# Output projection of a two-layer trunk: raw weight loads over five places, and splits placed behind the scaling of probabilities

## The chip, the cores and the metric

The kernel runs on one core of one Trainium2 chip. The metric is device time in microseconds (us): the median of several runs of the whole kernel. A core has a matrix engine (PE, whose weight loads are shown apart as PEld), a vector engine (DVE), a scalar engine (ACT), GpSimd (POOL) and SyncE (SP). Each of them works off its own list of instructions in the order in which they were issued. Here SP only starts transfers from main memory.

## The reference, cut to what matters

The model is a decoder trunk of two layers over 512 positions of width 1024. Each layer is half a SwiGLU block, a mixer with 8 forgetting-attention ("Fox") heads and 4 differential heads, and another half SwiGLU block. Everything is float32.

```python
for layer in range(DEPTH):
    x = x + 0.5 * _swiglu(_rmsnorm(x, ffn1_norm[layer]), ...)
    h = _rmsnorm(x, mix_norm[layer])
    proj = h @ w_in                       # 1024 x 3080
    o_f, o_d = _causal_block_attention(...)   # 8 Fox heads, 4 differential heads
    x = x + concat([o_f, o_d]) @ w_out    # 1024 x 1024, the product that the change is about
    x = x + 0.5 * _swiglu(_rmsnorm(x, ffn2_norm[layer]), ...)
return _rmsnorm(x, final_norm)
```

## The kernel before, in words

**Split weights.** A float32 product is made of three products of a rounded format. Each operand is split into a high part, which is the operand rounded, and a low part, which is what the rounding left out. `split` (L87 to L90) makes them from a raw block of 128 x 1024: ACT copies it (L88), then DVE subtracts (L89). `mm3` (L450 to L455) issues the three matrix products: high x high (L453), high x low (L454) and low x high (L455). So the first product of a block needs only ACT's part of the split, and the second needs DVE's part as well.

**The stream of weight blocks.** All weight blocks lie in one list, `stream`, in the order of their use. `plain` (L204 to L219) describes a block of the mixer: `need` starts the load of its raw block into a named place (`raw_tag`) if that place isn't marked busy, and `make` splits it and gives the place back. `ensure` (L259 to L270) makes the next block and then asks the following blocks for their loads, each of them if it lies fewer than `early` steps ahead (here 3). For each layer the list holds 24 blocks of the input projection and 7 blocks of the output projection, in the order `OUT_K = (4, 5, 6, 7, 0, 1, 2)`; block 3 is loaded apart in `out_rest` (L1153 to L1178), into place R2. Raw blocks rotate through three places, R0, R1 and R2 (L248). The seven output blocks have R1, R2, R0, R1, R2, R0, R1. Splits of blocks 4 to 7 go into the four tiles `XA0` to `XA3`, which hold the input of the input projection until its last products have read them. Splits of blocks 0 to 2 go into ring tiles ("wg").

**The mixer.** Twelve units are worked off one after the other, the four differential heads (units 0 to 3) and then the eight Fox heads (units 4 to 11). The loop over `s` (L1222 to L1244) has four steps for each unit. In step `s = 4u + i`, `softmax_step` makes the scores of unit u for the i-th block of 128 queries (PE, L948 and L949), masks them (DVE, L981) and takes the exponential (ACT, L983). After every second block of a Fox head the probabilities are scaled by the reciprocal of their sums (L988 to L994). ACT does it, except for the first two blocks of Fox heads 4 to 7, where DVE does it (L992). So each of those heads has one pair of scalings on ACT, of 128 x 384 and 128 x 512, in its fourth step. `trans_step` transposes the probabilities of the unit five steps back (PE, L1016; split by L1019 and L1020), and `pv_step` multiplies them with the values six steps back (PE, L1053 and L1054), and then adds up the head's output (L1083, L1084) and, at every second head, splits it (L1035, L1036).

**The filler.** Between these steps `pace` lets a generator, `filler`, issue other products of PE: the rest of the input projection and then `out_early` (L1135 to L1151). How far it may be after each third of a step is given by a table, counted in matrix products:

```python
LEAD = 70
TARGET = [128, 228, 280, 334, 380, 466, 478, 512, 520, 552, 564, 594, 612]
```

The n-th number is the count at the end of unit n. `out_early` takes the blocks of `w_out` in the order 4, 5, 6, 7, 0, 1 for three of the four groups of outputs of the first half of positions (9 products for each block), then the fourth group (18 products), then block 2 for all four groups (12). `take_wo` calls `next_w`, so a block's `make` runs where its first product is issued. What is left is issued after the loop (L1247), and then `out_rest` follows.

**What sets the order.** The program is written down in the order of these calls, and a scheduler then places the instructions of each engine: the earliest in this written order goes first, but one whose inputs are there (by the scheduler's reckoning) may be placed ahead of earlier ones that still wait. So a split or a filler product can move ahead of attention work. `tc.issue_after(x)` keeps the instructions of a block behind instruction x in the list of x's engine; it adds no wait.

**Other users of the places.** `w0` and `w1` hold the outputs of the differential heads (`os_`, L711; two heads in each) until `one` (L1102 to L1107) has read them with DVE (L1106).

Of the kernel before, what the change touches and what calls it, by code (L numbers as in the profile page):

```python
# [52 lines left out]
def rf(t):  # L53
    return t.bitcast(F32)
# [3 lines left out]
def trunk(ctx, tc, xT, x, gains, gain_row, w_gu, w_dn, w_in, w_ff, w_out, fbias, lams, subln, consts, rope, out):  # L58
    nc = tc.nc
    act, dve, pool, pe, sp = nc.scalar, nc.vector, nc.gpsimd, nc.tensor, nc.sync  # L60
# [16 lines left out]
    def home(tag, shape, dt, name):  # L77
        return sb.tile(shape, dt, tag=tag, name=name, bufs=1)
# [8 lines left out]
    def split(src, hi, lo):  # L87
        act.copy(out=hi, in_=src)  # L88
        dve.tensor_tensor(out=lo, in0=src, in1=rf(hi), op=ALU.subtract)  # L89
        return hi, lo  # L90
# [7 lines left out]
    def ring_tile(tag, cols):  # L98
        g = home(tag, [P, 2, 1024], F32R, "wg")
        return g[:, 0, :cols], g[:, 1, :cols]  # L100

    def raw_tile(tag, cols, src):
        t = home(tag, [P, 1024], F32, "raw")
        w = min(step[0], cols)
        for o in range(0, cols, w):
            sp.dma_start(out=t[:, o:o + w], in_=src[:, o:o + w])
        return t[:, :cols]
# [5 lines left out]
    stream = []  # L113
# [54 lines left out]
    def push(units, i, ring):  # L168
        for early, need, make in units:
            tag = ring[i % 5]  # L170
            i += 1
            stream.append((tag, early, need, lambda make=make, tag=tag: make(tag)))
        return i
# [27 lines left out]
            return tags.get(b), src  # L201
        return forms(order, 1, cols, where)

    def plain(src, raw_tag, tag):  # L204
        got = []

        def need():
            if not got and raw_tag not in busy:
                busy.add(raw_tag)
                got.append(raw_tile(raw_tag, 1024, src))  # L210

        def make():
            need()
            busy.discard(raw_tag)
            if tag is None:
                w = xt_[len_x.pop(0)]
                return split(got[0], w[:, 0:1024], w[:, 1024:2048])
            return split(got[0], *ring_tile(tag, 1024))
        return tag, 3, need, make  # L219

    NCH = len(PARTS_OF[0])

    def parts_of(n):

        parts = [("u", 0)]
        for c in range(1, NCH):
            parts += [("u", c), ("d", c - 1)]
        parts[-1] = ("dd", NCH - 1)
        return parts

    def pair_units(n):
        own = {s: iter(dn_units(n, NCH - 2 + i, "".join(u[0] for u in PAIRS[n] if u[1] == s), i == 1))
               for i, s in enumerate("ab")}
        return [next(own[u[1]]) for u in PAIRS[n]]

    def part_order(kind, c):
        return FIRST if (kind, c) == ("u", 0) else STEADY

    xt_ = [None] * KP
    len_x = list(range(KP)) * DEPTH  # L240
    OUT_K = (4, 5, 6, 7, 0, 1, 2)
    for n in range(2 * DEPTH):
        l = n // 2
        if n % 2 == 1:
            for i in range(24 + len(OUT_K)):
                k = OUT_K[i - 24] if i >= 24 else None
                tag = MIX[l][i % 3] if i < 24 else None if k >= 4 else MIX[l][(i - 28) % 3]
                stream.append(plain(w_in[l, i] if i < 24 else w_out[l, k], f"R{(i + 1) % 3}", tag))  # L248
        r = 0
        for kind, c in parts_of(n):  # L250
            if (n, kind, c) != (0, "u", 0):
                r = push(pair_units(n) if kind == "dd" else
                         (gu_units if kind == "u" else dn_units)(n, c, part_order(kind, c)), r, RINGS[n])
# [69 lines left out]
    norm = {}  # L323
# [357 lines left out]
    def mixer(l, n_next, mid):  # L681
# [14 lines left out]
        def pr_tile(u, qb):  # L696
            w = (qb + 1) * P
            return pg[u % 2][:, PR[qb]:PR[qb] + w]

        def pm_tile():  # L700
            return pg[nxt("pm", 2)][:, 1280:1792]
# [241 lines left out]
        def scores(q1, kk, m, qb, q2=None):  # L943
            n = (qb + 1) * P
            w = max(n, 256)
            p = psum("b")
            own = slice(qb * P, n)
            pe.matmul(p[:, 0:w], q1[m][:, own], kk[m][:, 0, 0:w], start=True, stop=False)  # L948
            pe.matmul(p[:, 0:w], (q1[m] if q2 is None else q2)[:, own], kk[m][:, 1, 0:w], start=False, stop=True)  # L949
            return p  # L950

        def softmax_step(u, qb):
            kind, h = units[u]
            n = (qb + 1) * P
            if kind == "d":
                st = sm.tile([P, 6], F32, tag="st", name="st", bufs=6)
                q1, kk = qk[("d", h)]
                pm = []
                for m in range(2):
                    p = scores(q1, kk, m, qb)  # L960
                    e = pr_tile(u, qb) if m == 0 else pm_tile()
                    dve.tensor_tensor_reduce(out=e[:, 0:n], in0=p[:, 0:n], in1=maskw[:, S - n:S], op0=ALU.add,
                                             op1=ALU.min, scale=1.0, scalar=3.0e38, accum_out=st[:, m:m + 1])
                    act.activation(out=e[:, 0:n], in_=e[:, 0:n], func=AF.Exp, scale=-1.0, bias=st[:, m:m + 1],
                                   accum_out=st[:, 2 + m:3 + m])
                    pm.append(e)
                dve.reciprocal(out=st[:, 4:6], in_=st[:, 2:4])
                dve.tensor_tensor(out=st[:, 5:6], in0=st[:, 5:6], in1=nlam, op=ALU.mult)
                act.mul(out=pm[1][:, 0:n], in_=pm[1][:, 0:n], mul=st[:, 5:6])
                dve.scalar_tensor_tensor(out=pm[0], in0=pm[0], scalar=st[:, 4:5], in1=pm[1][:, 0:n],  # L970
                                         op0=ALU.mult, op1=ALU.add)
                probs[u].append(pm[0])
            else:
                q1, kk = qk[("f", h // 2)]
                fox_q(h)
                p = scores(q1, kk, h % 2, qb, fq[h])
                e = pr_tile(u, qb)
                if qb % 2 == 0:
                    fst["st"] = sm.tile([P, 3, 2], F32, tag="st", name="st", bufs=6)
                st, i = fst["st"], qb % 2  # L980
                dve.tensor_tensor_reduce(out=e, in0=p[:, 0:n], in1=maskw[:, S - n:S], op0=ALU.add, op1=ALU.min,  # L981
                                         scale=1.0, scalar=3.0e38, accum_out=st[:, 0, i:i + 1])
                act.activation(out=e, in_=e, func=AF.Exp, scale=-1.0, bias=st[:, 0, i:i + 1],  # L983
                               accum_out=st[:, 1, i:i + 1])
                probs[u].append(e)
                if i == 0:
                    return
                dve.reciprocal(out=st[:, 2], in_=st[:, 1])  # L988
                for i in range(2):
                    e, r = probs[u][qb - 1 + i], st[:, 2, i:i + 1]  # L990
                    if h >= FOX_H // 2 and qb < 2:
                        dve.tensor_scalar(out=e, in0=e, scalar1=r, scalar2=None, op0=ALU.mult)  # L992
                    else:
                        act.mul(out=e, in_=e, mul=r)  # L994

        pts = {}

# [187 lines left out]
        early = [4, 5, 6, 7, 0, 1]  # L1185
# [28 lines left out]
        def fill_to(n):  # L1214
            while done[0] < n:
                w = next(fill, None)
                if w is None:
                    return
                done[0] += w
        fill_to(LEAD)  # L1220
        target = [LEAD] + TARGET
        for s in range(4 * len(units) + 5 + LAG):  # L1222
            u, i = divmod(s, 4)

            def pace(j):
                a = target[min(u, len(target) - 1)]
                b = target[min(u + 1, len(target) - 1)]
                fill_to(a + (b - a) * (3 * i + j) / 12)
            now, later[:] = list(later[:1]), later[1:]
            v, kb = divmod(s - 4 - LAG, 4)  # L1230
            if 0 <= v < len(units):
                trans_step(v, kb)
            pace(1)
            if u < len(units):
                softmax_step(u, i)
                if i == 1 and u + 1 < len(units) and units[u + 1][0] == "f":
                    fox_q(units[u + 1][1])
            pace(2)
            for f in now:
                f()  # L1240
            v, kb = divmod(s - 5 - LAG, 4)
            if 0 <= v < len(units):
                pv_step(v, kb)
            pace(3)  # L1244
        while later:
            later.pop(0)()
        run(fill)  # L1247
# [107 lines left out]
    w0 = []  # L1355
# [220 lines left out]
```

## Time and profile before

| what | value |
|---|---|
| runs of the kernel, us | 1827.43, 1827.82, 1830.53; median 1827.82 |
| profiled execution, us | 1829.35 |
| its span, first to last instruction, us | 1827.4 |
| mean granted clock of PE | 0.999 |
| PE, DVE, ACT busy, share of the span | 99%, 86%, 61% |
| bytes read from main memory | 283.33 MB |

The span is the time from the first to the last instruction of one profiled execution; about 2 us of that execution's time lie around it. A row of the timeline gives start (us from the start of the span), duration (us), engine, source line, operation, output tile <- input tiles, shape and count; a bracket behind it gives the idle time of the engine just before and what ended it. A start marked SPq is the issue of a transfer, not its landing. A row of the windows gives, for a stretch of time, the busy time and the number of instructions of each engine. The ends of matrix products are modelled, so their durations overlap: the pace of PE is read from starts or counts.

### The profile page before, as it was taken

The page shows a single profiled execution, that of the slowest core. Times are in us where ns is not written, and L with a number is a line of the kernel's source. Part 1 is how long each engine was busy: PE and PEld are TensorE (multiplying, and loading weights), DVE is VectorE, ACT ScalarE, POOL GpSimd, SP SyncE. Part 2 cuts the span into 40 slices and gives each one's busy share as a digit, 9 for nine tenths or more (in the row PEclk, how much of TensorE's full clock was granted, in tenths as well). Part 3 has the DMA queues.
Part 4 walks back from the last instruction along what each step waited for, and adds up shares of the span by engine and source line. Part 5 has one row for each costly group of instructions (what it writes and reads, how often), then busy time and mean ns, then how long its engine had stood idle before and what let it go on. Part 6 is the DMA issues. An engine that isn't in the chain of part 4 may idle for free.

```text
span 1827.4 us, 24309 instructions
## 1 busy us (share of the span) xinstructions
PE 1813.4 (99%) x8638; PEld 1493.3 (82%) x8638; DVE 1576.1 (86%) x2441; ACT 1120.4 (61%) x1780; POOL 134.2 (7%) x164
## 2 busy tenths in 40 slices
PE   9999999999999999999999999999999999999998
PEld 5888888878878888888888888898788788888887
DVE  7898899788695998899999898997787869898998
ACT  7555556557785745554676554565676856455555
POOL 2010000000000100000001000100000010000001
PEclk9999999999999999999999999999999999999999
DMA  9786664343345867767667767824333467776661
GB/s 308 218 228 184 178 183 129 105 127 100 116 122 158 206 200 187 193 161 196 163 188 209 183 162 195 207 75 123 112 108 102 136 162 198 206 201 179 161 179 58
DMA packets 93145, 301.80 MB, mean 165 GB/s; under 512 B 12568, under 2 KB 13080, under 8 KB 93024
## 3 DMA queue, kind: packets, MB, share of 16 engines
q1 hardware_dynamic: 72288, 229.89, 37.9%
q0 software_dynamic: 19296, 68.17, 21.7%
q10 hardware_dynamic: 1440, 2.19, 0.4%
q8 instruction: 68, 1.11, 0.3%
q14 instruction: 53, 0.43, 0.1%
HBM read 283.33 MB, written 2.20 MB: 156 GB/s over the span
## 4 chain that ended last, share of the span: by engine, by line
PE 88%; DVE 5%; ACT 4%; DMA 2%; issue 1%; SPq 0%; ACTq 0%; DVEq 0%; POOL 0%; POOLq 0%
PE ps_c L455 13%; PE ps_c L454 13%; PE ps_c L453 13%; PE ps L454 10%; PE ps L455 10%; PE ps L453 10%; PE ps_a L453 3%; PE ps_a L454 3%; PE ps_a L455 3%; PE ps_t L555 2%; PE ps_g L1389 2%; DVE wg L89 1%; ACT pg L983 1%; DMA rbd<-ms_d 1%; PE ps_t L372 1%
## 5 line engine op out<-in xcount | busy, mean ns | idle before, releaser
L88 ACT CAST wg<-raw 128x1024 fp32r<-128x1024 f32 (+1 forms) x525 | 540.0, 1032 | 491.8 <-PE ps_c L455 194.8
L89 DVE TENSOR_TENSOR wg<-raw,wg 128x1024 fp32r<-128x1024 f32 (+1 forms) x525 | 621.0, 1191 | 111.2 <-ACT wg L88 110.2
L453 PE MATMUL ps_c<-wg,xf 128*128 128x512 f32 (+1 forms) x736 | 277.1, 377 | 0.6 <-ACT xf L88 0.6
L455 PE MATMUL ps_c<-wg,xf 128*128 128x512 f32 (+1 forms) x736 | 276.3, 376 | 0.2 <-DVE xf L89 0.2
L454 PE MATMUL ps_c<-wg,xf 128*128 128x512 f32 (+1 forms) x736 | 276.3, 375 | 0.0
L453 PE MATMUL ps<-wg,xf 128*128 128x512 f32 (+1 forms) x552 | 210.2, 381 | 0.0
L454 PE MATMUL ps<-wg,xf 128*128 128x512 f32 (+1 forms) x552 | 207.4, 376 | 0.0
L455 PE MATMUL ps<-wg,xf 128*128 128x512 f32 (+1 forms) x552 | 207.1, 376 | 0.0
L453 PEld LDWEIGHTS ps_c<-wg,xf 128*128 128x128 f32 x736 | 138.5, 188 | 26.5 <-ACT xf L88 1.1
L455 PEld LDWEIGHTS ps_c<-wg,xf 128*128 128x128 f32 x736 | 138.5, 188 | 25.6 <-DVE xf L89 0.6
L454 PEld LDWEIGHTS ps_c<-wg,xf 128*128 128x128 f32 x736 | 138.5, 188 | 25.2 <-issue 0.2
L140 POOL DMA_DIRECT2D raw<-w_gu x86 | 74.6, 868 | 879.7 <-DMA raw<-w_gu 328.1
L453 PE MATMUL ps_c<-wg,hf 128*128 128x512 f32 x352 | 137.4, 390 | 0.0
L455 PE MATMUL ps_c<-wg,hf 128*128 128x512 f32 x352 | 137.1, 389 | 0.0
L454 PE MATMUL ps_c<-wg,hf 128*128 128x512 f32 x352 | 137.0, 389 | 0.0
L455 PEld LDWEIGHTS ps<-wg,xf 128*128 128x128 f32 x552 | 103.9, 188 | 18.9 <-DVE xf L89 0.2
L453 PEld LDWEIGHTS ps<-wg,xf 128*128 128x128 f32 x552 | 104.0, 188 | 17.7 <-ACT xf L88 0.2
L454 PEld LDWEIGHTS ps<-wg,xf 128*128 128x128 f32 x552 | 104.1, 189 | 17.5
L588 DVE SCALAR_TENSOR_TENSOR x<-ps_c,x 128x512 f32<-128x512 f32 x160 | 103.7, 680 | 0.8 <-PE ps_c L455 0.4
L453 PE MATMUL ps_a<-XA,wg 128*128 128x512 f32 x256 | 103.7, 405 | 0.1
L453 PE MATMUL ps<-wg,hf 128*128 128x512 f32 x264 | 103.4, 392 | 0.0
L454 PE MATMUL ps<-wg,hf 128*128 128x512 f32 x264 | 102.7, 389 | 0.0
(294 smaller groups left out, 3478.6 us busy)
## 6 DMA issues: line engine op xcount, KB each, us to landing
raw<-w_gu SPq DMA_DIRECT2D x218, 512.0 KB
raw<-w_dn SPq DMA_DIRECT2D x100, 512.0 KB
raw<-w_gu POOLq DMA_DIRECT2D x86, 512.0 KB, 6.9
raw<-w_in SPq DMA_DIRECT2D x48, 512.0 KB
raw<-w_dn POOLq DMA_DIRECT2D x40, 512.0 KB, 7.5
kdup<-qk_t SPq DMA_DIRECT2D x64, 128.0 KB
raw<-w_out SPq DMA_DIRECT2D x16, 512.0 KB
raw<-w_dn SPq DMA_DIRECT2D x20, 256.0 KB
```

The lines of the kernel that those rows point to most:

```text
L88: act.copy(out=hi, in_=src)
L89: dve.tensor_tensor(out=lo, in0=src, in1=rf(hi), op=ALU.subtract)
L140: pool.dma_start(out=t, in_=where(two, h)[1], accum_op=ALU.add)
L372: pe.transpose(p[:, e * 256 + j * P:e * 256 + (j + 1) * P], xs[2 * half + j][:, k * P:(k + 1) * P], ident)
L453: pe.matmul(p, lh, rh, start=start, stop=False, skip_group_check=again)
L454: pe.matmul(p, lh, rl, start=False, stop=False, skip_group_check=again)
L455: return pe.matmul(p, ll, rh, start=False, stop=stop, skip_group_check=again)
L555: pe.transpose(pj[j][:, e * 256 + p * P:e * 256 + (p + 1) * P], hs[j][p][:, o:o + P], ident)
L588: norm["upd"] = dve.scalar_tensor_tensor(out=xc, in0=src, scalar=scale, in1=xc, op0=ALU.mult, op1=ALU.add)
L983: act.activation(out=e, in_=e, func=AF.Exp, scale=-1.0, bias=st[:, 0, i:i + 1], accum_out=st[:, 1, i:i + 1])
L1389: pe.matmul(pg[2 * half + j], gained(kp, e, half)[:, j * P:(j + 1) * P], w0[kp][:, e * S:(e + 1) * S], start=kp + e == 0, stop=kp == KP - ...
```

## The change

The seven output blocks get the raw places R1, R2, w0, w1, R0, R1, R2, and are asked for five steps ahead where it was three. The instruction that scales probabilities on ACT is remembered as the newest one, and ACT's part of each output block's split is kept behind it in ACT's list. The memory of it is dropped at the end of the mixer's loop, before the rest of the filler is issued. The diff is whole but for its context lines:

```diff
-    def plain(src, raw_tag, tag):
+    def plain(src, raw_tag, tag, early=3):
...
             if tag is None:
                 w = xt_[len_x.pop(0)]
-                return split(got[0], w[:, 0:1024], w[:, 1024:2048])
-            return split(got[0], *ring_tile(tag, 1024))
-        return tag, 3, need, make
+                w = w[:, 0:1024], w[:, 1024:2048]
+            else:
+                w = ring_tile(tag, 1024)
+            with tc.issue_after(norm["scaled"]) if early > 3 and "scaled" in norm else nullcontext():
+                return split(got[0], *w)
+        return tag, early, need, make
...
     OUT_K = (4, 5, 6, 7, 0, 1, 2)
+    OUT_RAW = ("R1", "R2", "w0", "w1", "R0", "R1", "R2")
...
-                stream.append(plain(w_in[l, i] if i < 24 else w_out[l, k], f"R{(i + 1) % 3}", tag))
+                stream.append(plain(w_in[l, i] if i < 24 else w_out[l, k],
+                                    f"R{(i + 1) % 3}" if i < 24 else OUT_RAW[i - 24], tag, 3 if i < 24 else 5))
...
                     else:
-                        act.mul(out=e, in_=e, mul=r)
+                        norm["scaled"] = act.mul(out=e, in_=e, mul=r).ins
...
             pace(3)
+        norm.pop("scaled")
         while later:
             later.pop(0)()
         run(fill)
```

## The prediction

> **What bounds the kernel now.** I read the page first, then the windows of the stage that the change touches, then the chain of waits through that stage, then the timelines of ACT, PE, DVE and SP in it.
>
> ```profile
> span 1827.4 us, 24309 instructions
> ...
> PE 1813.4 (99%) x8638; PEld 1493.3 (82%) x8638; DVE 1576.1 (86%) x2441; ACT 1120.4 (61%) x1780; POOL 134.2 (7%) x164
> ...
> PE 88%; DVE 5%; ACT 4%; DMA 2%; issue 1%; SPq 0%; ACTq 0%; DVEq 0%; POOL 0%; POOLq 0%
> ```
>
> PE is busy for 1813.4 of 1827.4 us, so 14 us are idle in the whole span. The change neither adds nor removes a product: it can win only PE's idle time, and loses where PE idles more. In the windows (stretch, length, then busy time and count of PE, PEld, DVE, ACT, POOL; clock, DMA) the first two rows are the end of layer 0's attention, the next two the same places in layer 1, then a stretch of nothing but output products, then one of the SwiGLU block.
>
> ```profile
> 519.90:546.40 26.50, 26.22 (x142) 21.47 (x140) 25.29 (x68) 25.30 (x58) 0.00 (x0) 1.00 0.53 154
> 546.40:559.40 13.00, 12.37 (x66) 9.80 (x65) 7.77 (x15) 8.64 (x18) 1.72 (x2) 1.00 0.65 187
> 1424.70:1452.30 27.60, 26.42 (x141) 21.37 (x140) 25.24 (x68) 25.27 (x58) 0.00 (x0) 1.00 0.48 147
> 1452.30:1465.30 13.00, 12.37 (x65) 9.79 (x64) 7.80 (x15) 8.67 (x18) 0.86 (x1) 1.00 0.56 157
> 562.20:573.10 10.90, 10.90 (x49) 8.88 (x48) 1.77 (x3) 2.30 (x4) 1.73 (x2) 1.00 1.00 278
> 600.00:700.00 100.00, 100.00 (x459) 83.04 (x458) 91.35 (x118) 61.18 (x79) 9.55 (x11) 1.00 0.72 194
> ```
>
> From 519.9 to 546.4 three engines are full at once: PE 26.2, ACT 25.3 and DVE 25.3 of 26.5 us. PE idles 0.28 us there and 0.63 us to 559.4; in layer 1 it is 1.18 and 0.63. That is 2.7 us in all. One output product takes 10.9 / 48 = 0.227 us (the 49th had begun before). The chain of waits shows what sets the pace of the attention in layer 0 (start, length, engine, tile, line):
>
> ```profile
> 520.02 0.94 ACT XA L88
> ...
> 523.81 1.89 ACT XA L88 x2
> ...
> 527.29 1.12 ACT pg L994 x2
> ...
> 535.57 1.13 DVE XA L89
> ...
> 537.80 1.14 DVE wg L89
> 539.12 1.12 DVE wg L89
> ...
> 545.19 1.23 ACT pg L994 x2
> ```
>
> Splits of output blocks (L88, L89) hold 0.94 + 1.89 + 1.13 + 1.14 + 1.12 = 6.2 us of this chain: attention is paced by ACT and DVE, and PE stays full only because filler covers it. Here are ACT's rows with the splits and the scalings:
>
> ```profile
> 523.69 2.01 ACT L88 CAST XA<-raw 128x1024 fp32r<-128x1024 f32 x2
> ...
> 527.18 1.22 ACT L994 ACTIVATE pg<-pg,st 128x384 f32<-128x384 f32 x2
> ...
> 531.44 1.05 ACT L88 CAST XA<-raw 128x1024 fp32r<-128x1024 f32 x1
> ...
> 534.04 1.05 ACT L88 CAST wg<-raw 128x1024 fp32r<-128x1024 f32 x1
> ...
> 535.73 1.03 ACT L88 CAST wg<-raw 128x1024 fp32r<-128x1024 f32 x1
> ...
> 536.81 1.23 ACT L994 ACTIVATE pg<-pg,st 128x384 f32<-128x384 f32 x2
> ...
> 540.84 1.05 ACT L88 CAST wg<-raw 128x1024 fp32r<-128x1024 f32 x1
> ...
> 545.19 1.23 ACT L994 ACTIVATE pg<-pg,st 128x384 f32<-128x384 f32 x2
> ```
>
> The scalings are those of Fox heads 4, 5 and 6 (units 8, 9, 10). Block 4 is split at 520.0 (chain), 5 and 6 at 523.69, 7 at 531.44, 0 at 534.04, 1 at 535.73, 2 at 540.84. Six blocks are split before head 6 is scaled.
>
> **Part one: where the pin puts each split.** The scaling that counts is the newest one written down when the block is made. The filler counts 48 products for each of the six projections left to it, 96 for each of the two value projections and 16 for the gates, so out_early starts at 544, and a block follows every 9: 4 at 544, 5 at 553, 6 at 562, 7 at 571, 0 at 580, 1 at 589. The targets run 520 to 552 over unit 9, to 564 over unit 10, to 594 over unit 11. Count 544 is passed in unit 9's fourth step, before that step's softmax, so the newest scaling is head 4's. 553 is passed in unit 10's first step: head 5's. 562 is passed at the end of unit 10's fourth step, after its softmax, 571 and 580 in unit 11 before its scaling: head 6's for blocks 6, 7 and 0. 589 comes after unit 11's softmax: head 7's. Block 2 is made after the loop and is free. So blocks 6, 7, 0 and 1 go from before head 6's scaling to behind it; 4 and 5 stay before it, but behind the scalings of heads 4 and 5, where both are now ahead of head 4's. What that moves on PE, out of 519.95 to 546.4 (L453 rows; L454 and L455 have as many):
>
> ```profile
> L453 PE MATMUL ps_a<-XA,y 128*128 128x512 f32 x12 | 4.5, 414 | 0.0
> ...
> L453 PE MATMUL ps_a<-wg,y 128*128 128x512 f32 x6 | 2.1, 396 | 0.0
> ```
>
> Today 3 x (12 + 6) = 54 filler products of blocks 4 to 1 run before head 6's scaling is done. Pinned, only 4 and 5 can: 18. So 36 x 0.227 = **8.2 us** of PE work goes behind that point, in each layer.
>
> **Part two: how much sooner the scaling comes.** With fewer splits in its way the chain shortens. At most it loses all 6.2 us of splits and ACT's idle 1.2 us (26.5 less 25.3): 7.4. At least, if blocks 4 and 5 sit on it again with ACT's 0.95 (half the step of the pair at 523.69) and DVE's 1.1 each, 6.2 - 4.1 = 2.1. No row says which; I take the middle, 4.7.
>
> **Part three: the sum.** Today 13.0 us follow the scaling's end until 559.4, where what is left of the filler is PE's alone: 12.4 of work, 0.6 idle. Pinned, that work is 12.4 + 8.2 = 20.6 and starts 4.7 us sooner. The 0.6 of idling goes, since filler abounds there. Block 6's products wait for its split behind the scaling, 0.95 on ACT and 1.1 on DVE; transposes of head 6 and products of head 5 cover part, so between 0 and 2.0, and I take 0.5, as most of PE's list is ready then. Layer 0: 8.2 - 4.7 - 0.6 + 0.5 = **+3.4**. Layer 1 has one wait more:
>
> ```profile
> 1441.79 1.05 ACT L88 CAST wg<-raw 128x1024 fp32r<-128x1024 f32 x1 [1.18 <-DMA raw<-w_out]
> 1442.74 1.22 ACT L994 ACTIVATE pg<-pg,st 128x384 f32<-128x384 f32 x2
> ```
>
> ```profile
> 1441.54 0.50 PE L454 MATMUL ps_a<-XA,y 128*128 128x512 f32 x1 [0.28 <-DVE XA L89]
> ...
> 1442.11 0.40 PE L454 MATMUL ps_a<-XA,y 128*128 128x512 f32 x1
> 1443.40 0.44 PE L1016 MATMUL ps_b<-ident,pg 128*128 128x128 f32 x2 [0.90 <-ACT pg L994]
> ```
>
> Block 1's split waits 1.18 us on ACT for its load, head 5's scaling is queued behind it, and PE's transposes wait for the scaling. This the change does remove: the split now follows head 7's scaling. So layer 1's chain shortens by 1.2 more: **+2.2**. Together **+5.6 us**. By the ends: 8.2 - 7.4 - 0.6 and 1.2 less in layer 1 give -0.8 for both; 8.2 - 2.1 + 2.0 and 1.2 less give +15.0.
>
> **Part four: the loads.** SP's rows for w_out, and DVE's last readings of the differential outputs in layer 0:
>
> ```profile
> 497.83 0.33 SPq L106 DMA_DIRECT2D raw<-w_out  x1
> ...
> 522.45 0.36 SPq L106 DMA_DIRECT2D raw<-w_out  x1
> ...
> 532.07 0.53 SPq L106 DMA_DIRECT2D raw<-w_out  x1
> ...
> 536.76 0.36 SPq L106 DMA_DIRECT2D raw<-w_out  x1
> 539.01 0.36 SPq L1156 DMA_DIRECT2D raw<-w_out  x1
> ```
>
> ```profile
> 501.91 0.74 DVE L1106 SCALAR_TENSOR_TENSOR ou<-o,sub_s,rbd 128x512 f32<-128x512 f32 x1
> 505.36 0.75 DVE L1106 SCALAR_TENSOR_TENSOR ou<-o,sub_s,rbd 128x512 f32<-128x512 f32 x1 [0.31 <-DMA rbd<-ms_d]
> ```
>
> Block 6 now loads at 497.83 and 7 at 522.45. After: block 0 takes R0 near 498, 6 takes w0 once two heads' outputs are read, near 502, 7 takes w1 behind the last reading, near 506; 1 and 2 follow the splits of 4 and 5 out of R1 and R2. Loads in w0 and w1 wait on SP, and what is written behind them there (copies of keys and queries) could wait too; SP is idle most of that time and an issue is 0.3 to 0.5 us, so 0, or 1 us with that cover gone. Block 3 moves to the end: its R2 is free only after block 2's split. It is issued at 539.01 now, and its products come last, behind the 12.4 us of work of the second window; a load issued some 5 us later still has 10 us or more. Zero.
>
> [...] In the saturated stretch from 562.2, PEld is busy 8.88 of 10.9 us, 81%; in the stage, 21.47 of 26.5, also 81%. [...]
>
> **The rivals.** First: the chain shortens by nearly all it can, 7 us, since ACT and DVE lose four splits each and attention needs no filler to go on. Then 8.2 - 7 - 0.6 + 0.5 is +1.1 in layer 0 and -0.1 in layer 1: **+1**, no change. For it: three splits in a row of the chain are ACT's own. Against it: exponentials, scalings and transposes hang together through PE, ACT and DVE, and block 4 and 5 stay. Second, on the other side: PE finds other work while the pinned splits wait. The fourth group of blocks 4 and 5 (6 products, 1.4 us a layer) runs early if a bank is free for it; with the chain 7.4 us shorter nothing new stands idle, and the 2.7 us of today's waits go, with the part that the modelled ends hide. In layer 1, L1016 starts at 1443.40, and the product before it, from 1442.11, holds PE for 0.227: 1.06 lost, where the row says 0.90. So 0.16 is hidden, some 0.8 over five waits. That is **-3.5**, 1824.3. It decides from a shortening of about 8 us on. PE does not run that group early at 546.2, where it idles:
>
> ```profile
> 547.54 0.51 PE L1053 MATMUL ps_b<-pair,vf 128*128 128x512 f32 x1 [0.63 <-ACT pair L1019]
> ```
>
> Third: the chain does not shorten, because PE or DVE paces it where ACT is freed: 8.2 - 2.1 in each layer and block 6's wait, with the terms of part three +10 to +15. Fourth: the pin binds nothing, as the scheduler keeps the old order anyway: 0; the row of block 6 at 523.69, 21 us before head 6's scaling, speaks against it.
>
> **How the numbers follow.** The forecast has 0.52, the first rival 0.25, the second 0.15, the third 0.06, the fourth 0.02. The sum is made against the profiled execution's 1829.35 us (span 1827.4 and 1.95 around it), which is 1.5 above the median; +5.6 on the median gives **1833.4**. A measurement of this kernel tells 0.2%, or 3.7 us, from no change. Of the forecast 0.43 lies above that and 0.09 below it; with the third rival, slower has 0.49. Same has 0.09 + 0.25 + 0.05 + 0.02 = 0.41, faster the second rival's other 0.10. The range, 1825.5 to 1839.5 (-2.3 to +11.7), takes in the first rival and most of the forecast's ends, and leaves out the faster part of the second and the far end of the third. The forecast's own range is 1830 to 1838.
>
> **What would show it.** Right: each L88 of block 4 and 5 directly behind a 384 and 512 pair of L994, those of 6, 7 and 0 behind head 6's pair; 18 and not 54 filler products before it; that pair 3 to 7 us sooner; PE idle by some 3 us more in each layer between the last projection and it, waiting for L1019, L994 or L88. All w_out loads but two issued by 507 in layer 0, and no ACT wait on w_out. Wrong: PE's idle in the two windows no larger than now, filler of the fourth group between heads 4 and 6, or the pair of head 6 more than 8 us sooner.

## The result: 0.76% slower, more than the range allowed

The changed kernel takes 1842.75 us (median of four runs, 1842.48 to 1842.99), the kernel before 1828.34 (1827.43 to 1830.53) beside it: a ratio of 1.0076, 95% interval 1.0064 to 1.0089, or +14.4 us. The forecast was +5.6 (1833.4), its range ended at 1839.5. The profiled execution took 1842.99, 13.6 more than that of before. In the changed file lines shift by five: L453 is now L458, the scaling L994 is L999, the transposes of probabilities L1016 are L1021, ACT's and DVE's copies of them L1024 and L1025, the products behind them L1058 and L1059.

The page of the changed kernel, the lines that answer to those of before:

```profile
span 1841.2 us, 24312 instructions
...
PE 1821.0 (99%) x8638; PEld 1496.5 (81%) x8638; DVE 1577.6 (86%) x2441; ACT 1121.0 (61%) x1780; POOL 134.2 (7%) x164
```

The number of products is the same, 8638, but the span is 13.8 longer. PE's idle time is the span less its busy time: 14.0 before, 20.2 now. That is 6.2 of the 13.8. The other 7.6 stand in PE's *busy* time, 1813.4 before and 1821.0 now, though there is no more to compute. So the same products took longer.

Where: two windows of the kernel before (layer 0 and 1, from the last stretch of attention to the first transposes of the next phase) and the same two of the changed kernel. Columns are as in the prediction; the last but two is the granted clock.

```profile
519.90:573.15 53.25, 52.33 (x265) 42.31 (x264) 37.04 (x87) 37.29 (x79) 3.45 (x4) 1.00 0.68 194
1424.70:1479.12 54.42, 52.61 (x265) 42.23 (x264) 38.25 (x88) 37.30 (x79) 3.45 (x4) 1.00 0.64 189
```

```profile
519.90:580.68 60.78, 56.38 (x260) 43.57 (x259) 37.21 (x83) 36.04 (x76) 3.46 (x4) 0.94 0.55 157
1432.20:1492.39 60.19, 55.23 (x259) 42.67 (x258) 38.41 (x84) 35.99 (x76) 3.46 (x4) 0.97 0.54 157
```

The two stretches grew by 7.5 and 5.8 us, 13.3 together: the whole loss is here. Idle time grew from 0.92 to 4.40 and from 1.81 to 4.96, which is +3.5 and +3.2. The granted clock fell to 0.94 and 0.97. A finer cut of the changed kernel into windows of 3.41 us, as long as layer 1's stretch of half clock, shows where:

```profile
539.75:543.16 3.41, 1.69 (x10) 0.97 (x8) 3.38 (x13) 3.36 (x11) 0.00 (x0) 1.00 0.14 28
543.16:546.57 3.41, 3.06 (x8) 2.03 (x9) 2.55 (x3) 3.41 (x7) 0.00 (x0) 0.50 0.33 126
546.57:549.99 3.42, 3.42 (x10) 2.65 (x9) 2.89 (x4) 1.46 (x3) 0.00 (x0) 0.50 0.00 0
549.99:553.40 3.41, 3.41 (x16) 2.79 (x15) 0.00 (x0) 0.00 (x0) 0.00 (x0) 1.00 0.48 157
1454.52:1457.93 3.41, 2.03 (x8) 1.10 (x9) 2.57 (x5) 3.41 (x6) 0.00 (x0) 1.00 0.48 154
1457.93:1461.34 3.41, 3.41 (x9) 2.62 (x9) 3.38 (x5) 2.36 (x5) 0.00 (x0) 0.50 0.00 0
```

A window in which PE had work for 1.69 (2.03) of 3.41 us is followed by 6.83 (3.41) us at a granted clock of 0.50. In half clock the filler that should catch up runs slower: 10 products in the window from 546.57, 16 in the next. PE's timeline shows both, the wait and the pace (start, length, what it is; idle time before it in brackets):

```profile
542.65 0.44 PE L1021 MATMUL ps_b<-ident,pg 128*128 128x128 f32 x2 [1.65 <-ACT pg L999]
...
544.20 1.65 PE L458 MATMUL ps_a<-XA,y 128*128 128x512 f32 x3 [0.25 <-ACT XA L88]
...
546.50 0.63 PE L459 MATMUL ps_a<-XA,y 128*128 128x512 f32 x1
546.93 0.63 PE L460 MATMUL ps_a<-XA,y 128*128 128x512 f32 x1
...
550.43 0.39 PE L458 MATMUL ps_a<-XA,y 128*128 128x512 f32 x1
550.66 0.40 PE L459 MATMUL ps_a<-XA,y 128*128 128x512 f32 x1
```

PE stands idle for 1.65 us for head 6's scaling. Then output products start 0.43 us apart (546.50 and 546.93) where from 550.43 on it is 0.23. In the 3.41 us before the clock fell in layer 0, PE was busy for 1.69, and its longest pause was 1.65 us.

Taken at the granted 0.50, half of the length of these stretches is lost where PE is full, so by its length half clock costs 6.83 / 2 + 3.41 / 2 = 5.1 us. This is an estimate: 0.43 us from start to start where it was 0.23 is 1.9 times as long (what else speaks for and against this size comes with `busy_pe` below). So 6.6 of idling and 5.1 of half clock make 11.7 of the 13.3; 1.6 are left in PE's busy time, to which I come back.

The total of PE's waits, the first rows of the changed kernel (sum, times, longest):

```profile
PE ps_b L1021 <- ACT pg L999: 5.1, 8, 1.6
PE ps_a L458 <- ACT XA L88: 1.7, 4, 0.5
PE ps_b L1058 <- ACT pair L1024: 1.1, 2, 0.6
```

Before, the first of these was a single wait of 0.9. Transposes of probabilities that wait for the scaling are now the largest wait. ACT's splits and scalings in layer 0 (heads 4, 5, 6, 7 are scaled at 524.55, 531.85, 541.99 and 557.61):

```profile
524.55 1.21 ACT L999 ACTIVATE pg<-pg,st 128x384 f32<-128x384 f32 x2
528.52 1.06 ACT L88 CAST XA<-raw 128x1024 fp32r<-128x1024 f32 x1
...
531.85 1.23 ACT L999 ACTIVATE pg<-pg,st 128x384 f32<-128x384 f32 x2
532.98 1.03 ACT L88 CAST XA<-raw 128x1024 fp32r<-128x1024 f32 x1
538.72 1.05 ACT L88 CAST wg<-raw 128x1024 fp32r<-128x1024 f32 x1
541.99 1.23 ACT L999 ACTIVATE pg<-pg,st 128x384 f32<-128x384 f32 x2
543.12 1.98 ACT L88 CAST XA<-raw 128x1024 fp32r<-128x1024 f32 x2
546.37 1.05 ACT L88 CAST wg<-raw 128x1024 fp32r<-128x1024 f32 x1
554.55 1.06 ACT L88 CAST wg<-raw 128x1024 fp32r<-128x1024 f32 x1
557.61 1.23 ACT L999 ACTIVATE pg<-pg,st 128x384 f32<-128x384 f32 x2
558.74 1.04 ACT L88 CAST wg<-raw 128x1024 fp32r<-128x1024 f32 x1
```

Block 4 is split at 528.52, 5 at 532.98, the free block 2 at 538.72, blocks 6 and 7 at 543.12, 0 at 546.37, 3 at 554.55 and 1 at 558.74.

### The profile page after: what moved, and what is told of

Same layout as the page of the kernel before. It is cut to its first block, busy times and chain, and to the rows that moved or that the text cites. A ratio compares the mean times of both kernels' runs of the same rounds, so it can differ in the third digit from the quotient of the medians.

```text
span 1841.2 us, 24312 instructions
## 1 busy us (share of the span) xinstructions
PE 1821.0 (99%) x8638; PEld 1496.5 (81%) x8638; DVE 1577.6 (86%) x2441; ACT 1121.0 (61%) x1780; POOL 134.2 (7%) x164
## 3 DMA queue, kind: packets, MB, share of 16 engines
q0 software_dynamic: 19296, 68.17, 21.2%
## 4 chain that ended last, share of the span: by engine, by line
PE 90%; DVE 4%; ACT 4%; issue 1%; DMA 1%; SPq 0%; DVEq 0%; ACTq 0%
PE ps_c L460 13%; PE ps_c L459 13%; PE ps_c L458 13%; PE ps L458 10%; PE ps L460 10%; PE ps L459 10%; PE ps_a L459 4%; PE ps_a L458 4%; PE ps_a L460 4%; PE ps_t L560 2%; PE ps_g L1395 2%; PE ps_b L1021 1%; DVE wg L89 1%; PE ps_t L377 1%; ACT pg L988 1%
## 5 line engine op out<-in xcount | busy, mean ns | idle before, releaser
L88 ACT CAST wg<-raw 128x1024 fp32r<-128x1024 f32 (+1 forms) x525 | 540.0, 1032 | 490.0 <-PE ps_c L460 194.9
L458 PE MATMUL ps_c<-wg,xf 128*128 128x512 f32 (+1 forms) x736 | 277.1, 377 | 0.5 <-ACT xf L88 0.5
L458 PE MATMUL ps<-wg,xf 128*128 128x512 f32 (+1 forms) x552 | 210.4, 382 | 0.0
L458 PEld LDWEIGHTS ps_c<-wg,xf 128*128 128x128 f32 x736 | 138.5, 188 | 26.5 <-ACT xf L88 0.9
L458 PE MATMUL ps_c<-wg,hf 128*128 128x512 f32 x352 | 137.4, 390 | 0.0
L458 PEld LDWEIGHTS ps<-wg,xf 128*128 128x128 f32 x552 | 104.0, 188 | 17.7 <-ACT xf L88 0.2
L458 PE MATMUL ps_a<-XA,wg 128*128 128x512 f32 x256 | 103.8, 405 | 0.1
L458 PE MATMUL ps<-wg,hf 128*128 128x512 f32 x264 | 103.4, 392 | 0.0
```

The costliest lines, as they stand in the source:

```text
L458: pe.matmul(p, lh, rh, start=start, stop=False, skip_group_check=again)
```

## The experiments

**Theory.** The pin takes filler products away from the places where attention leaves PE without work. PE then idles, and a window with little work is followed by half clock, which makes the loss larger than the idling. **Rival one** (theory 2 in the expectations): the places and the earlier loads cost something (SP's order, buffers). **Rival two** (theory 3 there): the splits as such, standing behind scalings, hold up what ACT has to do next, so that any pinned split costs its own share wherever its products go. Each ratio below is to the kernel before on the same chip; "held" is the number of filler products that a pin takes from before head 6's transposes, worked out from the order of the filler.

**The places and loads alone** (`loads_only`), the pin left out:

```diff
-            with tc.issue_after(norm["scaled"]) if early > 3 and "scaled" in norm else nullcontext():
-                return split(got[0], *w)
+            return split(got[0], *w)
```

> The new places and the five steps ahead, without the pin. Theory 1 (the pin holds back filler products, PE idles and its clock is halved for a while): nothing is held back, so the time is that of the kernel before, 1824 to 1829 us, less up to 2 us since no split waits for its load any more; the granted clock stays 1.00 through both attention stages. Theory 2 (the places cost it: the loads in w0 and w1 and block 3's load behind block 2's split hold up SP or the last products): 1838 us or more, as the changed kernel.

Measured: 1828.68 beside 1828.45, ratio 0.9999 (0.9991 to 1.0008). No cost and no gain: rival one falls. Where did the waits of before go? Two rows of ACT, then one of PE:

```profile
527.48 1.03 ACT L88 CAST XA<-raw 128x1024 fp32r<-128x1024 f32 x1
528.41 1.22 ACT L998 ACTIVATE pg<-pg,st 128x384 f32<-128x384 f32 x2
```

```profile
529.08 0.44 PE L1020 MATMUL ps_b<-ident,pg 128*128 128x128 f32 x2 [1.04 <-ACT pg L998]
```

ACT no longer waits for loads of w_out. But block 7 now comes earlier and its split takes ACT ahead of head 4's scaling, and PE waits 1.04 us for that. In layer 0 that wait and one of 0.18 stand where the kernel before had 0.28 and 0.63: the old waits gave way to new ones.

**The pin alone** (`pin_only`), the raw places and steps of before:

```diff
-    OUT_RAW = ("R1", "R2", "w0", "w1", "R0", "R1", "R2")
+    OUT_RAW = ("R1", "R2", "R0", "R1", "R2", "R0", "R1")
...
-                if i < early and running:
+                if i < (3 if early == 5 else early) and running:
```

> The pin on the old places R0 to R2, three steps ahead. Theory 1: as the changed kernel or worse, 1840 to 1848 us, with half clock in both attention stages, since the same 36 products wait behind head 6's scaling and the loads of blocks 0, 1 and 2 now follow late splits. Theory 2: 1826 to 1831 us.

Measured: 1840.65, ratio 1.0067 (1.0054 to 1.0079), an interval that overlaps the whole change's. The pin is the cost. Two of its windows:

```profile
524.44:527.85 3.41, 1.82 (x11) 1.03 (x10) 2.79 (x11) 3.27 (x9) 0.00 (x0) 1.00 0.39 85
527.85:531.26 3.41, 3.41 (x13) 2.96 (x13) 3.41 (x7) 3.41 (x8) 0.00 (x0) 0.50 0.40 85
```

Half clock comes four times here, 3.41 us each, 6.8 us of loss by its length. PE's idle time is 18.3, 4.3 more than before: together 11.1 of the 12.2 by which the profiled span is longer.

**The pin one head earlier** (`older_pin`): the same constraint, but behind a scaling two places older than the newest.

```diff
-            with tc.issue_after(norm["scaled"]) if early > 3 and "scaled" in norm else nullcontext():
+            with tc.issue_after(scaled[-3]) if early > 3 and len(scaled) > 2 else nullcontext():
...
+    scaled = []
...
-                        norm["scaled"] = act.mul(out=e, in_=e, mul=r).ins
+                        scaled.append(act.mul(out=e, in_=e, mul=r).ins)
...
-        norm.pop("scaled")
+        scaled.clear()
```

> The changed kernel with each block's split kept behind the scaling one head older than the newest. By the written order blocks 6, 7 and 0 then follow head 5's scaling and block 1 head 6's, so only 9 products (2.0 us) and not 36 are held behind head 6's. Theory 1: 1827 to 1833 us, and no half clock. Theory 2: as the changed kernel, 1838 us or more.

Measured: 1830.00, ratio 1.0007 (0.9998 to 1.0016), and the clock is 1.00 through both stages. ACT scales twice for each head (384 and 512 elements), so two places back is one head. The expectation's count did not come true: 36 products of the output blocks, and not 45 of the 54, run before head 6's scaling ends (543.3 in layer 0). But block 0's split lies ahead of that scaling (539.13), so its products are ready when it ends and start at 543.63. A constraint on the order costs nothing by itself; it depends on which scaling it names, and on whether filler is ready where PE would wait.

**More work for PE** (`busy_pe`): the changed kernel with twelve more products a layer in the stretch where PE idles. They are score products whose result is overwritten, so this adds work that the reference does not ask for.

```diff
-        def scores(q1, kk, m, qb, q2=None):
+        def scores(q1, kk, m, qb, q2=None, extra=0):
...
+            for _ in range(extra):
+                pe.matmul(p, q1[m][:, own], kk[m][:, 0], start=True, stop=False, skip_group_check=True)
...
-                p = scores(q1, kk, h % 2, qb, fq[h])
+                p = scores(q1, kk, h % 2, qb, fq[h], 3 if (h, qb) in ((6, 3), (7, 0), (7, 1), (7, 2)) else 0)
```

> The changed kernel with 12 redundant score products for each layer (128 x 512, for the last step of head 6 and the first three of head 7; each is overwritten by the score product proper, so nothing else changes): 24 x 0.227 = 5.4 us more work for PE. If the half clock comes from PE's idling and costs what the records show (some 5 us in both layers), it stays at 1.00 and the time is the changed kernel's or lower, 1837 to 1843 us. If the idling alone costs and the clock has nothing to do with it, 1842 to 1848 us, with half clock as before.

Measured: 1838.59, ratio 1.0055 (1.0042 to 1.0067). With 24 x 0.227 = 5.4 us more to compute it is 4.2 us *faster* than the changed kernel, and in the profiled executions 1841.2 - 1837.9 = 3.3 faster. The same windows as above:

```profile
520.90:578.64 57.74, 55.16 (x271) 43.72 (x270) 38.47 (x84) 36.37 (x74) 3.46 (x4) 1.00 0.58 169
1430.70:1489.44 58.74, 56.15 (x275) 44.44 (x275) 39.48 (x89) 37.32 (x77) 3.46 (x4) 1.00 0.57 163
```

The clock is 1.00 in both, and PE's waits for the scaling fell from 5.1 us to 1.5. PE's idle time fell from 20.2 to 1837.9 - 1820.9 = 17.0. Had the added work only filled idle time, it would have cost 5.4 - 3.2 = 2.2; it gained 3.3, so 5.5 came from elsewhere, and the half clock, 5.1 by its length, is what went away. The chain up to head 6's scaling did not get shorter by as much: counted from the layer's first transposes, the scaling comes 0.8 us sooner in layer 0 and 0.1 later in layer 1. This is the run that shows the clock as a cost of its own.

Its size is less sure. One execution of each kernel is profiled, but every run's span and mean clock are on record. With block 6 alone pinned (below), one run at 0.995 has a span of 1842.4 us, three at 0.997 have 1838.9 to 1839.9: 3.0 longer, where 0.002 x 1840 = 3.7 would be lost by the same reckoning. But two runs of `pin_only` at 0.998 (1838.4 and 1838.8) are only 1.2 and 0.8 us shorter than the profiled one at 0.995 (1839.6), where the reckoning gives 5.5, or 3.7 at the least that the rounding of these clocks allows. The mean also takes in the end of each execution, where PE has no work left and the clock is at 0.50 (from 1823.9 us on in the kernel before, from 1836.8 in the changed one), so these differences are rough. The 5.1 us are best read as an upper estimate; why `pin_only` gains less is open.

**The same work in the kernel before** (`busy_before`): the same edit, without the change.

> The control for the redundant products: the same 24 of them (12 a layer, overwritten, nothing else changed) in the kernel before, whose PE has no idle time there to take them. Theory 1: they cost nearly their whole time, 24 x 0.227 = 5.4 us, so 1832.5 to 1835 us, with the clock at 1.00. If such products are free in any case (and so say nothing in the changed kernel), 1828 to 1830 us.

Measured: 1832.21, ratio 1.0020 (1.0010 to 1.0029), +3.6 us. Here the added products cost what of them finds no idle time: PE's idle time fell from 14.0 to 1830.5 - 1818.9 = 11.6, and 5.4 - 2.4 = 3.0. That is a little less than was expected, as more of them found idle time. Of the two kernels in which they were tried, they help only the one where the pin has taken the filler.

**One block pinned at a time.** Four kernels with the new places, in each of which one block alone is pinned; the diff is that of block 6, the others name another `k`.

```diff
-    def plain(src, raw_tag, tag, early=3):
+    def plain(src, raw_tag, tag, early=3, only=False):
...
-            with tc.issue_after(norm["scaled"]) if early > 3 and "scaled" in norm else nullcontext():
+            with tc.issue_after(norm["scaled"]) if only and "scaled" in norm else nullcontext():
...
-                                    f"R{(i + 1) % 3}" if i < 24 else OUT_RAW[i - 24], tag, 3 if i < 24 else 5))
+                                    f"R{(i + 1) % 3}" if i < 24 else OUT_RAW[i - 24], tag, 3 if i < 24 else 5, k == 6))
```

> The new places, and the pin for block 6 alone (behind head 6's scaling); the six other splits are free. The products of blocks 7, 0 and 1 add into the same banks behind those of block 6, so 36 products wait for one split. Theory 1 (what costs is the filler that is held back): as much is held as in the changed kernel but only one split leaves the chain, so it is as slow or slower, 1842 to 1850 us, with half clock in both layers. Rival theory 3 (what costs is where the splits themselves lie, four of them crowding in behind head 6's scaling): one split moved costs a quarter, 1829 to 1833 us.

> As the last, for block 7 alone: 27 products are held behind head 6's scaling. Theory 1: less than with block 6 by 9 products a layer (2 x 2.0 us) and by some of the half clock, 1837 to 1844 us. Theory 3: as with block 6, 1829 to 1833 us.

> As the last, for block 0 alone: 18 products are held behind head 6's scaling. Theory 1: 1832 to 1838 us, and the clock may stay at 1.00. Theory 3: 1829 to 1833 us.

> The new places, and the pin for block 1 alone, which puts its split behind head 7's scaling: 9 products are held, and not behind head 6's scaling but head 7's, near the end of attention, with nothing held before. Theory 1: 1828.5 to 1832 us, clock at 1.00, so that the time rises from 0 products held (1828.7) over 9 to 18 (1833.3), 27 (1839.5) and 36 (1841.5).

Blocks are consumed in order, so a pin on one holds the products of all behind it. The traces bear the counts out: before head 6's scaling ends, 45, 36, 27 and 18 products run with block 1, 0, 7 and 6 pinned, where the kernel before has 54 (and `loads_only` 50). Idle time and half clock are those of the profiled execution:

| pinned | held a layer | median us | ratio (95%) | PE idle us | half clock us |
|---|---|---|---|---|---|
| none (`loads_only`) | 0 | 1828.68 | 0.9999 (0.9991 to 1.0008) | 14.5 | 0 |
| block 1 | 9 | 1830.22 | 1.0009 (0.9999 to 1.0018) | 16.0 | 0 |
| block 0 | 18 | 1833.26 | 1.0025 (1.0016 to 1.0035) | 16.7 | 3.4 |
| block 7 | 27 | 1839.52 | 1.0058 (1.0044 to 1.0071) | 21.2 | 6.8 |
| block 6 | 36 | 1841.50 | 1.0073 (1.0059 to 1.0086) | 21.7 | 6.8 |
| all (the change) | 36 | 1842.75 | 1.0076 (1.0064 to 1.0089) | 20.2 | 10.2 |

Time rises with the held products, and one pinned split (block 6) costs as much as all, within the intervals; its 1841.50 is just below the 1842 to 1850 that were expected. Rival two falls: it would have given each split its own share, with the sum at the whole. The rise is not even: up to nine products a layer cost 1.6 us, not told apart from nothing, and from 18 to 27 the step is 6 us, where idling and half clock both jump. The count at one point is not the whole of it either: `older_pin` has as many products before head 6's scaling as block 0 alone pinned (36) and costs nothing that can be told, since its next filler is ready when the scaling ends. With block 0 pinned, PE waits 0.86 us for the scaling at 544.72 and 0.50 for block 0's split at 546.26 in layer 0. PE's timeline with block 6 alone pinned shows the same wait as the changed kernel's:

```profile
544.53 0.44 PE L1021 MATMUL ps_b<-ident,pg 128*128 128x128 f32 x2 [1.39 <-ACT pg L999]
```

**A pin that should help** (`block7_head4`): of the pins only block 7's, behind head 4's scaling, since in `loads_only` this split stood in front of it.

```diff
-            with tc.issue_after(norm["scaled"]) if early > 3 and "scaled" in norm else nullcontext():
+            with tc.issue_after(scaled[-5]) if only and len(scaled) > 4 else nullcontext():
```

`scaled` is the list of `older_pin`, and `only` is set for block 7 alone.

> The new places, no pin but one: block 7's split is kept behind head 4's scaling, in front of which it lies without a pin, and PE loses 1.2 us there in each layer. Nothing else is held. Theory 1: the 1.2 us go, in part, 1826 to 1828.5 us where the new places alone give 1828.7; a gain that small may not be told from none. Theory 3 makes no difference here.

Measured: 1827.83, ratio 0.9996 (0.9987 to 1.0005): not told from the kernel before. The profile says why:

```profile
527.04 1.03 ACT L88 CAST wg<-raw 128x1024 fp32r<-128x1024 f32 x1
527.98 1.22 ACT L1000 ACTIVATE pg<-pg,st 128x384 f32<-128x384 f32 x2
532.04 1.07 ACT L88 CAST XA<-raw 128x1024 fp32r<-128x1024 f32 x1
```

```profile
528.64 0.44 PE L1022 MATMUL ps_b<-ident,pg 128*128 128x128 f32 x2 [1.04 <-ACT pg L1000]
```

Block 7 moved to 532.04, and block 0, which nothing pins here, took its place ahead of the scaling. The wait of 1.04 us is the same. No version that beats the kernel before by more than its measurement tells was found.

## Why the prediction was wrong in its size

**What held.** Part one: the order of the splits is the one worked out there, block by block, 6, 7 and 0 behind head 6's pair and 1 behind head 7's. Before head 6's transposes the changed kernel has 18 filler products of the output blocks:

```profile
L459 PE MATMUL ps_a<-XA,y 128*128 128x512 f32 x6 | 2.6, 432 | 0.3 <-DVE XA L89 0.3
L460 PE MATMUL ps_a<-XA,y 128*128 128x512 f32 x6 | 2.4, 396 | 0.0
...
L458 PE MATMUL ps_a<-XA,y 128*128 128x512 f32 x6 | 1.8, 410 | 0.5 <-ACT XA L88 0.5
```

So 36 were held and 8.2 us went behind. Part four: the loads cost nothing. SP's rows in the changed kernel:

```profile
497.91 4.14 SPq L106 DMA_DIRECT2D raw<-w_out  x2
...
508.06 0.33 SPq L106 DMA_DIRECT2D raw<-w_out  x1
```

Block 0 is loaded at 497.91 and 6 behind it in the same row, 7 at 508.06 (2 us later than worked out, and 1 us past the mark of 507), and 1, 2 and 3 at 531.00, 535.29 and 541.59, in time. ACT waits for no load of w_out, and `loads_only` shows the zero by its time. The forecast's kind of loss, the held filler left without cover by a chain that shortens too little, was right, and so were its marks: PE idles some 3 us more in each layer (3.5 and 3.2 measured), waiting for L999, L88 and L1024, and head 6's pair comes 3 to 7 us sooner (3.3 and 4.4, as follows).

**What was too large: part two.** Head 6's scaling was to come 4.7 us sooner in layer 0 and 5.9 in layer 1. In layer 0 it starts at 541.99 where it was 545.19, and the layer began 0.1 later, so 3.3. In layer 1:

```profile
1454.24 1.23 ACT L999 ACTIVATE pg<-pg,st 128x384 f32<-128x384 f32 x2
```

Before it was 1451.11, but the layer itself (its first transposes) began at 1234.81 and now at 1242.30, 7.5 later: so 4.4 sooner. That is 1.4 + 1.5 = 2.9 us less than the middle value that was taken. The 1.2 us by which layer 1 was to gain more are right (4.4 - 3.3 = 1.1). The chain of waits of the changed kernel shows what still holds it in layer 0 (start, length, engine, tile, line):

```profile
528.64 0.36 ACT XA L88
...
533.08 0.94 ACT XA L88
534.04 1.24 DVE XA L89
...
538.81 0.95 ACT wg L88
```

These splits of blocks 4, 5 and 2 hold 3.5 us of it, where 6.2 were held before: 2.7 less. Blocks 4 and 5 were in the working's lower end. Block 2 was not: the prediction says that six blocks are split before head 6 is scaled, but its own rows show seven, and the seventh, the free block 2, now lies on the chain, between head 5's scaling and head 6's, with 0.95. From the end of head 6's scaling to the end of the stretch (before in both layers, then the changed kernel):

```profile
546.42:573.15 26.73, 26.10 (x125) 20.84 (x124) 11.73 (x20) 11.98 (x23) 3.45 (x4) 1.00 0.83 234
1452.34:1479.12 26.78, 26.15 (x126) 20.85 (x124) 12.97 (x21) 11.99 (x22) 3.45 (x4) 1.00 0.81 233
```

```profile
543.22:580.68 37.46, 37.17 (x159) 29.55 (x160) 16.29 (x24) 15.60 (x26) 3.46 (x4) 0.91 0.69 202
1455.47:1492.39 36.92, 36.06 (x159) 28.67 (x160) 17.55 (x25) 15.61 (x27) 3.46 (x4) 0.95 0.67 203
```

PE's work behind the scaling grew by 11.1 and 9.9 us; less the half clock's 3.4 and 1.7 that is 7.7 and 8.2, where the prediction had 8.2. Idle time behind it changed by -0.3 and +0.2, where the prediction had -0.1 (0.5 less 0.6). So two of the three terms came out, and only the shortening was mis-sized: with the measured terms the sum is 7.7 - 3.3 - 0.3 and 8.2 - 4.4 + 0.2, together 8.1, and what was measured without the half clock is 13.3 - 5.1 = 8.2.

**What was missing: the clock in part three.** The sum took idle time at its own length and every product after it at 0.227, so the price of a slower clock stood at nothing, without a reason given. No row of before shows a clock other than 1.00 in the stage, and the prediction let that stand for a kernel that idles more. Idle time of 1.65 us in one piece, with smaller pieces around it, was followed by 3.41 or 6.83 us at a granted clock of 0.50, with output products 0.43 us apart and not 0.23, and this was just the stretch in which PE's list is full and the held work is caught up. By its length it cost an estimated 5.1 us, 3.4 in layer 0 and 1.7 in layer 1. It is the larger of the two faults, but neither alone carries the time out of the range, which ended at 1839.5: 1833.4 + 2.9 is 1836.3 and 1833.4 + 5.1 is 1838.5. With both it is 1841.4.

The third rival named +10 to +15, and +14.4 falls there, but not by its mechanism: the chain did shorten, by 3.3 and 4.4 us. The first and second rival needed 7 us and more.

**What is left.** 1.6 of the 13.3 us lie in PE's busy time and are neither idling nor half clock; in `busy_pe` it is about 2.1 (7.5 more busy time, 5.4 of it added work). The prediction saw that modelled ends hide 0.16 us for each wait; the changed kernel has 19 waits in the two stretches where before had five, and 14 x 0.16 = 2.2 would be of this size. This is argued, not tested.

## What to carry to other kernels

Filler that is moved away from a stretch paced by other engines does not only leave its own length idle there: price the idle share of each few microseconds, since eleven windows here with 1.48 to 2.03 us of work in 3.41 were followed by 3.4 or 6.8 us at half clock (0.50), and it hit the work that was to make good the loss. When an order is pinned, count the products queued behind the pinned step, not the step (one block in front cost as much as all), and ask whether other filler is ready where the engine would wait. And when a wait is removed, look at what the freed instruction then stands in front of: here the earlier split took the place of the late load.

## What the runs showed of the hardware

In these runs the clock fell without a long pause. In the attention stages half clock (0.50) set in eleven times, in five of the profiled kernels, and each time PE had been busy for 1.48 to 2.03 of the 3.41 us before it, in pieces, with no pause above 1.65. Windows of the changed kernel with 2.18 to 2.84 of work were not followed by it. (The kernel before and the changed one also end at 0.50, from 1823.9 and 1836.8 on, after PE's last product, which starts at 1818.93 and 1832.57; PE has no work left there, and this is left out.) The busy time alone does not part them, though: these windows with block 6 and with block 7 pinned were followed by full clock:

```profile
541.68:545.09 3.41, 1.90 (x14) 1.34 (x12) 2.20 (x13) 2.93 (x9) 0.00 (x0) 1.00 0.34 126
536.18:539.59 3.41, 1.98 (x11) 1.23 (x9) 3.41 (x10) 3.14 (x8) 0.00 (x0) 1.00 0.32 106
```

Nor does the number of products: these hold 14 and 11, and those that were followed by half clock 7 to 11. What parts them stays open. So does why half clock lasted 6.83 us in layer 0 of the changed kernel, where it lasted 3.41 us in layer 1 and in each of the nine other cases.
